# A hybrid transformer block on one core: the retention heads' gate columns and value columns change places in the program

## The chip, the cores and the metric

The kernel runs on one core of one Trainium2 chip. The metric is device time in microseconds (us) of one execution, given as the median of several runs. The engines are TensorE (PE, its weight loads shown as PEld), VectorE (DVE), ScalarE (ACT), GpSimd (POOL) and SyncE (SP). Each works through its own list of instructions in order, and semaphores make one wait for another; transfers are put in queues by SP and by ACT.

## The reference, cut to what matters

1024 latent tokens and 256 context tokens of width 1024 are normalised, modulated and projected by one matrix. Its columns go to two groups of heads:

```
p = h @ w_in                       # 1280 tokens x 4112 columns
qkv_a, z, ab, rq, rk, rv, rg = split(p)
# group A, gated delta rule: q, k, v after a 5-tap convolution and silu
q, k, v = silu(conv(qkv_a));  g = -exp(A) * softplus(a + dt);  beta = sigmoid(b)
o_gdn = rms_norm(delta(q,k,v,g) + delta_backward(...)) * silu(z)
# group B, retention: rotary on rq and rk, none on rv
o_ret = group_norm(ret(rq,rk,rv) + ret_backward(...)) * silu(rg)
x = x + g1 * (concat(o_gdn, o_ret)[latents] @ w_out)
x = x + g2 * swiglu(modulate(rms_norm(x)))
return rms_norm(x)
```

The columns rv (retention's values) are needed for all 1280 tokens, since the context's state starts the scan; the gates rg and z are needed for the latent tokens alone. Both have 512 columns, as have rk, rq and z. The 16 columns ab hold the decay and write strengths a and b of the delta rule and are needed for all tokens.

## The kernel before, in words

Each f32 operand is split into a high and a low part, and each product takes three matmuls. Tokens lie in 10 tiles of 128: tiles 0 and 1 are the context, tiles 2 to 9 the latents. A *token-major* product gives 128 tokens by 256 columns: `tm_half` (L367 to L373) issues 12 matmuls for half of the 1024 inputs, and a tile takes 24 in all. Ten groups of 256 columns are named by `GROUPS`, two to a name: groups 0 and 1 are rv, 2 and 3 rk, 4 and 5 rq, 6 and 7 rg, 8 and 9 z. Group 0 is 272 wide, because the 16 columns ab ride along; `tm_store` evacuates them to `xa` (L384), the rest to `res` (L402 or L532), and stores it in HBM. A *convolution block* (`conv_block`, L611 to L624) gives 128 columns by all tokens: 8 times 3 matmuls for each chunk of 256, 512 and 512 tokens, then two copies on ACT, shifted sums on DVE and a Silu on ACT.

The program's stages, with the microseconds of the profiled execution:

- 0 to 111, stage 1: the modulation's first rows, the norms (square root on ACT, L126), the transposes `xtr`, and groups 0 and 1 for all ten tiles, in the order of the tile groups 2-3, 4-5, 6-9, 0-1. Their evacuation is a plain copy. The PSUM banks for `tm` are three ("pa").
- 111 to 253: convolution blocks 4 to 7 (k) and 0 to 3 (q), with k's transposes `kt` for its norms. DVE runs `ada_rest` (sums `acc` over weights that SP loads, then a matmul `gr`, L504) and the softplus chain from `xa` to `g`; PE sums it up by `G` (L582) and transposes it by `GT` (L595). The result is needed for every chunk's decay.
- Groups 6 and 7 (rg, latents only, Silu on ACT) are written behind q. Their 384 matmuls lie in PE's list from 121 to 276.
- 277 to 377, preparation of the ten chunks: `pre(t)` loads k and q (`kc`, `qc`), multiplies them on PE (`kk` L705, `qt` L710, `kq` L715), loads the decay row `gw`, masks it on POOL, takes four exps on ACT (L726), and multiplies on DVE. `invert` runs 62 small steps on DVE for four chunks at once. Between these lie the convolution blocks 8 to 11 (v); each is followed by ten transposes `vT` (L856) of its result `y`, which ACT scales into `vt` (L859) and stores.
- 377 to 474: group 8 (z's first half) and the merges of the inverted blocks.
- After that the delta scan with groups 2 to 5 and 9 among it, the retention scan, the output projection and the feed-forward part, the last 750 us of it with PE busy nearly throughout.

The order of the instructions on each engine is not the order of the code. The code is written stage by stage, and a scheduler that works from estimated times moves the instructions of one stage between those of another wherever dependencies and buffers allow it; token-major groups fill PE's list in this way. Once compiled, each list is fixed.

Buffers matter too. Pool W holds the weights of the convolution blocks and of the late token-major groups (two buffers of each kind); pool W2, which is closed ahead of the preparation, holds those of group 1 and of rg.

Of the kernel before, what the change touches and what calls it, by code (L numbers as in the profile page):

```python
# [11 lines left out]
AF = mybir.ActivationFunctionType  # L12
# [13 lines left out]
H = 4  # L26
# [2 lines left out]
EPS = 1e-6  # L29
NEG = -200.0  # L30
FAR = -1e30
GROUPS = ["rv", "rk", "rq", "rg", "z"]


class Stop(Exception):
# [3 lines left out]
def build(nc, tc, ap, dbg=None, stop=None, marks=None):  # L39
    root = ExitStack()  # L40
    V, S, G, T, SY = nc.vector, nc.scalar, nc.gpsimd, nc.tensor, nc.sync

    def pool(name, bufs=1, side=None, space=None):
        kw = {}
        if side is not None:
            kw["side"] = side
        if space is not None:
            kw["space"] = space
        if space is not DRAM:
            kw["reuse_waits"] = "tile"  # L50
        es = ExitStack()
        p = es.enter_context(tc.tile_pool(name=name, bufs=bufs, **kw))
        root.push(es)
        p_close[id(p)] = es
        return p
# [3 lines left out]
    def close(p):  # L59
        p_close.pop(id(p)).close()  # L60
# [5 lines left out]
    def checkpoint(name):  # L66
        if dbg is not None:
            marks.append((name, int(nc.cur_bb.bb.instructions[-1].name.split("-")[-1])))
        if stop == name:
            raise Stop()  # L70
# [16 lines left out]
    def bank(tag, name):  # L87
        return PS["pool"].tile([P, 512], F32, tag=tag, name=name, bufs=PS["tags"][tag])

    def bank_a(name):  # L90
        return bank("pa", name)
# [99 lines left out]
    try:  # L191
# [20 lines left out]
        W = pool("w", bufs=2)  # L212
# [18 lines left out]
        WIDE = 272  # L231
        W2 = None
# [7 lines left out]
        def load_x(t):  # L240
            xts[t] = P0.tile([P, D], F32, tag="xt", name="xt", bufs=7)
            in_order(xts[t], ap["ctx"][t * P:(t + 1) * P, :] if t < 2 else ap["x"][(t - 2) * P:(t - 1) * P, :])
# [117 lines left out]
        def tm_weights(g, kh, pl, q=S):  # L360
            return weights(ap["wt"][g, :, 4 * kh:4 * kh + 4, :], [4, 256], V, pl, q, raws.get((g, kh)), g == 0)

        def tm_bank(g):
            return bank_a("tm")[:, 0:WIDE if g == 0 else 256]

        def tm_half(o, w, kh, t):

            tsl = slice(t * P, (t + 1) * P)
            whi, wlo = w
            for k in range(4 * kh, 4 * kh + 4):  # L370
                T.matmul(o, hhi[:, k, tsl], whi[:, k % 4, :], start=(k == 0), stop=False)  # L371
                T.matmul(o, hhi[:, k, tsl], wlo[:, k % 4, :], start=False, stop=False)  # L372
                T.matmul(o, hlo[:, k, tsl], whi[:, k % 4, :], start=False, stop=(k == KT - 1))  # L373
# [2 lines left out]
        zd = dr.tile([LT, P, 512], F32, tag="zd", name="zd")  # L376
        RD = {"rk": 0, "rq": 1, "rv": 2, "rg": 3}

        def tm_store(g, t, o, finish, store, pl):
            early = g < 2  # L380
            res = (W2 if early else R1).tile([P, 256], F32, tag="res", name="res", bufs=4 if early else 2)
            finish(t, o[:, 0:256], res)
            if g == 0:
                S.activation(xa[:, t, :], o[:, 256:WIDE], AF.Copy)  # L384
            nm, c0 = GROUPS[g // 2], (g % 2) * 256
            dst = zd[t - 2, :, c0:c0 + 256] if nm == "z" else rd[t, :, RD[nm], c0:c0 + 256]
            store.dma_start(dst, res)

        def token_major(g, tiles, finish, store, pl, q=S):

            w = [tm_weights(g, kh, pl, q) for kh in range(2)]

            for p in range(0, len(tiles), 2):
                pair = [(t, tm_bank(g)) for t in tiles[p:p + 2]]
                for kh in range(2):
                    for t, o in pair:
                        tm_half(o, w[kh], kh, t)
                for t, o in pair:
                    tm_store(g, t, o, finish, store, pl)

        def fin_copy(t, o, res):
            S.activation(res, o, AF.Copy)  # L402

        load_x(2)
        load_x(3)
# [18 lines left out]
        wr = {(0, 0): tm_weights(0, 0, W)}  # L424
# [22 lines left out]
        W2 = pool("w2", bufs=2)  # L447
        xa = W2.tile([P, TT, 16], F32, tag="xa", name="xa", bufs=1)
# [11 lines left out]
            hold = modulate(xnT[:, k, :], k, 0, slice(2 * P, 4 * P))  # L460
        normalize(1, hold)
        for gi, grp in enumerate(XGROUPS):
            for g in range(2):
                if gi == 0 and g == 1:
                    for kh in range(2):
                        wr[1, kh] = tm_weights(1, kh, W2)
                for t in grp:
                    if (g, t) in first:
                        o = first[g, t]
                    else:  # L470
                        o = tm_bank(g)
                        tm_half(o, wr[g, 0], 0, t)
                    tm_half(o, wr[g, 1], 1, t)
                    tm_store(g, t, o, fin_copy, S, W2)
                if g == 0 and gi + 1 < len(XGROUPS):
                    hold = modulated(gi + 1)
            if gi + 2 < len(XGROUPS):
                normalize(gi + 2, hold)
# [40 lines left out]
        def fin_rope(t, o, res):  # L519
# [7 lines left out]
                V.tensor_tensor(r4[:, :, a, :], o4[:, :, 1 - a, :], bc(sin, [P, 2, 64], 1), ALU.mult)  # L527
            for a, op in ((0, ALU.subtract), (1, ALU.add)):
                G.tensor_tensor(r4[:, :, a, :], ra[:, :, a, :], r4[:, :, a, :], op)

        def fin_gate(t, o, res):
            S.activation(res, o, AF.Silu)  # L532

        LAT, ALL = list(range(2, TT)), list(range(2, TT)) + [0, 1]
        for g in range(2):
# [66 lines left out]
        def conv_block(b, y, lat):  # L602

            whi, wlo = weights(ap["wg"][b], [KT, P], G if b % 2 else V, W, SY if b in (4, 5) else S)
            u = CV.tile([P, NTOK], F32, tag="u", name="u", bufs=2)
            for c0, n in (CHUNKS[1:] if lat else CHUNKS):
                ps = bank_c("b2")
                o = ps[:, :n]
                for k in range(KT):
                    hh, hl = hhi[:, k, c0:c0 + n], hlo[:, k, c0:c0 + n]  # L610
                    T.matmul(o, whi[:, k, :], hh, start=(k == 0), stop=False)  # L611
                    T.matmul(o, whi[:, k, :], hl, start=False, stop=False)  # L612
                    T.matmul(o, wlo[:, k, :], hh, start=False, stop=(k == KT - 1))  # L613
                S.activation(u[:, c0:c0 + n], o, AF.Copy)
                S.activation(y[:, c0:c0 + n], o, AF.Copy, scale=cw[:, b, 2:3])
            segs = [(NCTX, NLAT)] if lat else [(0, NCTX), (NCTX, NLAT)]
            for i, e in ((0, V), (1, V), (3, V), (4, V)):
                for s0, n in segs:
                    sh = i - 2
                    lo, hi = s0 + max(0, -sh), s0 + n - max(0, sh)  # L620
                    e.scalar_tensor_tensor(y[:, lo:hi], u[:, lo + sh:hi + sh], cw[:, b, i:i + 1], y[:, lo:hi],
                                           ALU.mult, ALU.add)
            a0 = NCTX if lat else 0
            S.activation(y[:, a0:], y[:, a0:], AF.Silu)  # L624

        def newy():
            return CV.tile([P, NTOK], F32, tag="y", name="y", bufs=3)
# [27 lines left out]
        for h in range(H):  # L655
            y = newy()
# [20 lines left out]
        for h in range(H):  # L677
            y = newy()
# [4 lines left out]
                        y[:, NCTX:].rearrange("p (t j) -> p t j", j=P))  # L683

        checkpoint("q")
        for g in (6, 7):
            token_major(g, LAT, fin_gate, S, W2, SY)
        checkpoint("rg")
        close(R2)
        close(W2)  # L690
        GU = pool("gu")
# [149 lines left out]
        def solve(b):  # L841
            for t in BATCH[b]:
                pre(t)
            checkpoint("pre%d" % b)
            invert(b)
            checkpoint("inv%d" % b)

        solve(0)
        solve(1)
        for h in range(H):  # L850
            y = newy()
            conv_block(8 + h, y, False)
            for t0, n in ((0, 2), (2, 4), (6, 4)):
                ps = bank_a("vT")
                for t in range(t0, t0 + n):
                    T.transpose(ps[:, (t - t0) * P:(t - t0 + 1) * P], y[:, t * P:(t + 1) * P], ident)  # L856
                vt = CV.tile([P, 4, P], F32, tag="vt", name="vt", bufs=2)
                for t in range(n):
                    S.activation(vt[:, t], ps[:, t * P:(t + 1) * P], AF.Copy, scale=sv3[:, t0 + t, h:h + 1])  # L859
                S.dma_start(vd[t0:t0 + n, :, h, :].rearrange("t p j -> p t j"), vt[:, :n])  # L860
        close(CV)
        checkpoint("v")
        RP = pool("rp", side="right")
# [12 lines left out]
        merge(2)  # L876


        for g in (8, 9):
            token_major(g, LAT, fin_gate, S, W)  # L880
        checkpoint("rgz")
        close(GM)
        close(G2)
# [374 lines left out]
        for i, l in enumerate(pairs):  # L1258
            y = nxt
# [194 lines left out]
        w = {}  # L1454
# [156 lines left out]
def prepare(inputs):  # L1611
# [13 lines left out]
    col = {"z": 1536, "rq": 2064, "rk": 2576, "rv": 3088, "rg": 3600}  # L1625
    wt = np.concatenate([w_in[:, col[n]:col[n] + 512] for n in GROUPS], 1)
    a["wt"] = f(wt.reshape(KT, P, 10, 256).transpose(2, 1, 0, 3))
# [27 lines left out]
```

## Time and profile before

| what | value |
|---|---|
| median of three runs | 1479.91 us (1479.66 to 1481.7) |
| the profiled execution | 1477.96 us |
| its span, first to last instruction | 1476.2 us |
| PE busy | 1397.2 us, 95% |
| DVE, ACT, POOL busy | 964.6, 614.0, 590.3 us |
| instructions | 24111, of them 8919 on PE |
| moved by DMA | 298.14 MB, 202 GB/s over the span |

The page gives busy times over the whole span and then the span in 40 slices, with a digit for each engine's tenths. The table of windows cuts it at given times. A row of the waits names the engine, what waits, `<-` what released it, and then the total, the count and the longest in us. In a timeline a row has its start, its length, the engine and the line of the program, then what is written `<-` what is read, and in square brackets the idle time ahead of it. "issue" is time in which the engine waited for nothing that the profile shows. Matmul records of f32 operands appear twice, since such a product takes two passes.

### The profile page before, as it was taken

The page shows a single profiled execution, that of the slowest core. Times are in us where ns is not written, and L with a number is a line of the kernel's source. Part 1 is how long each engine was busy: PE and PEld are TensorE (multiplying, and loading weights), DVE is VectorE, ACT ScalarE, POOL GpSimd, SP SyncE. Part 2 cuts the span into 40 slices and gives each one's busy share as a digit, 9 for nine tenths or more (in the row PEclk, how much of TensorE's full clock was granted, in tenths as well). Part 3 has the DMA queues.
Part 4 walks back from the last instruction along what each step waited for, and adds up shares of the span by engine and source line. Part 5 has one row for each costly group of instructions (what it writes and reads, how often), then busy time and mean ns, then how long its engine had stood idle before and what let it go on. Part 6 is the DMA issues. An engine that isn't in the chain of part 4 may idle for free.

```text
span 1476.2 us, 24111 instructions
## 1 busy us (share of the span) xinstructions
PE 1397.2 (95%) x8919; PEld 1199.2 (81%) x8919; DVE 964.6 (65%) x1856; ACT 614.0 (42%) x1326; POOL 590.3 (40%) x501
## 2 busy tenths in 40 slices
PE   7999999986789999899799899999999999999997
PEld 2898888975689999898688688877888888788885
DVE  6566789289792435689676877556555564657477
ACT  5643564587333111245443623233333332444445
POOL 0120010243202344234144688898555552335321
PEclk9999999998899999999899999999999999999999
DMA  9536686688888625996532265674222242776863
GB/s 337 197 105 205 189 249 200 219 264 277 282 216 277 238 76 178 416 341 209 184 125 104 97 238 210 242 264 162 105 97 105 107 151 79 260 260 194 288 216 114
DMA packets 170421, 298.14 MB, mean 202 GB/s; under 512 B 43496, under 2 KB 93880, under 8 KB 165952
## 3 DMA queue, kind: packets, MB, share of 16 engines
q1 hardware_dynamic: 118752, 253.17, 50.2%
q10 hardware_dynamic: 49072, 35.83, 7.8%
q0 software_dynamic: 2480, 7.60, 1.4%
q8 instruction: 70, 1.15, 0.3%
q14 instruction: 47, 0.39, 0.1%
HBM read 206.60 MB, written 89.96 MB: 201 GB/s over the span
## 4 chain that ended last, share of the span: by engine, by line
PE 55%; POOL 6%; DMA 5%; DVE 4%; issue 2%; ACT 2%; SPq 1%; ACTq 0%; POOLq 0%; DVEq 0%
PE ffn L1344 7%; PE ffn L1342 6%; PE ffn L1343 6%; PE fo L1470 4%; PE fo L1469 4%; PE fo L1468 4%; PE tm L371 3%; PE tm L373 3%; PE tm L372 3%; PE op L1203 2%; PE op L1201 2%; PE op L1202 2%; DMA wd<-tw 2%; POOL ws L1315 1%; DMA pk<-sd 1%
## 5 line engine op out<-in xcount | busy, mean ns | idle before, releaser
L371 PE MATMUL tm<-whi,hhi 128*128 128x256 f32 (+1 forms) x704 | 199.5, 287 | 7.7 <-ACT vt L859 3.4
L372 PE MATMUL tm<-wlo,hhi 128*128 128x256 f32 (+1 forms) x704 | 199.3, 285 | 2.4 <-issue 2.0
L373 PE MATMUL tm<-whi,hlo 128*128 128x256 f32 (+1 forms) x704 | 197.7, 285 | 0.0
L371 PEld LDWEIGHTS tm<-whi,hhi 128*128 128x128 f32 x704 | 132.8, 190 | 11.8 <-ACT vt L859 3.6
L1342 PE MATMUL ffn<-t,whi 128*128 128x512 f32 x352 | 136.9, 390 | 1.3 <-ACT whi L344 1.3
L1344 PE MATMUL ffn<-t,wlo 128*128 128x512 f32 x352 | 137.0, 390 | 1.0 <-DVE wlo L345 1.0
L1343 PE MATMUL ffn<-t,whi 128*128 128x512 f32 x352 | 137.0, 389 | 0.0
L372 PEld LDWEIGHTS tm<-wlo,hhi 128*128 128x128 f32 x704 | 133.7, 190 | 2.1 <-issue 0.9
L373 PEld LDWEIGHTS tm<-whi,hlo 128*128 128x128 f32 x704 | 132.8, 190 | 2.6 <-issue 1.8
L344 ACT ACTIVATE whi<-wraw 128x512 fp32r<-128x512 f32 (+2 forms) x98 | 75.1, 771 | 141.4 <-PE ffn L1343 80.5
L344 ACT ACTIVATE whi<-ws 128x512 fp32r<-128x512 f32 x88 | 55.6, 632 | 171.5 <-PE ffn L1343 123.4
L345 DVE TENSOR_TENSOR wlo<-ws,whi 128x512 fp32r<-128x512 f32 x88 | 93.9, 1068 | 47.0 <-ACT whi L344 46.8
L1469 PE MATMUL fo<-wlo,ahi 128*128 128x512 f32 x308 | 120.2, 390 | 2.1 <-DVE wlo L345 2.1
L1468 PE MATMUL fo<-whi,ahi 128*128 128x512 f32 x308 | 119.3, 390 | 0.7 <-ACT ahi L344 0.7
L1470 PE MATMUL fo<-whi,alo 128*128 128x512 f32 x308 | 119.0, 390 | 0.0
L345 DVE TENSOR_TENSOR wlo<-wraw,whi 128x512 fp32r<-128x512 f32 (+2 forms) x92 | 99.4, 1082 | 24.6 <-ACT whi L344 24.6
L1342 PE MATMUL ffn<-b,whi 128*128 128x512 f32 x264 | 103.8, 393 | 4.4 <-ACT whi L344 4.4
L1344 PE MATMUL ffn<-b,wlo 128*128 128x512 f32 x264 | 103.6, 393 | 0.8 <-DVE wlo L345 0.8
L1343 PE MATMUL ffn<-b,whi 128*128 128x512 f32 x264 | 103.4, 392 | 0.0
L612 PE MATMUL b<-hlo,whi 128*128 128x512 f32 (+1 forms) x256 | 94.4, 369 | 0.0
L613 PE MATMUL b<-hhi,wlo 128*128 128x512 f32 (+1 forms) x256 | 94.3, 368 | 0.0
L611 PE MATMUL b<-hhi,whi 128*128 128x512 f32 (+1 forms) x256 | 94.3, 368 | 0.0
(446 smaller groups left out, 3448.1 us busy)
## 6 DMA issues: line engine op xcount, KB each, us to landing
adaw<-ada SPq DMA_DIRECT2D x48, 512.0 KB, 4.4
pk<-sd SPq DMA_DIRECT2D x16, 1536.0 KB, 10.0
wraw<-wfi SPq DMA_DIRECT2D x44, 512.0 KB, 3.7
ar<-ad SPq DMA_DIRECT2D x33, 512.0 KB, 4.7
w<-wfo SPq DMA_DIRECT2D x22, 512.0 KB, 5.7
wd<-tw SPq DMA_DIRECT2D x11, 1024.0 KB, 4.8
ad<-act SPq DMA_DIRECT2D x20, 512.0 KB, 3.0
raw<-wd SPq DMA_DIRECT2D x20, 512.0 KB, 4.9
```

What stands on the lines that cost most here:

```text
L344: S.activation(hi, raw, AF.Copy)
L345: e.tensor_tensor(lo, raw, hi.bitcast(F32), ALU.subtract)
L371: T.matmul(o, hhi[:, k, tsl], whi[:, k % 4, :], start=(k == 0), stop=False)
L372: T.matmul(o, hhi[:, k, tsl], wlo[:, k % 4, :], start=False, stop=False)
L373: T.matmul(o, hlo[:, k, tsl], whi[:, k % 4, :], start=False, stop=(k == KT - 1))
L612: T.matmul(o, whi[:, k, :], hl, start=False, stop=False)
L1342: T.matmul(o, whi[:, k, :], xhi(xn, slice(0, 4), k), start=(first and k == 0), stop=False, **kw)
L1343: T.matmul(o, whi[:, k, :], xlo(xn, slice(0, 4), k), start=False, stop=False, **kw)
L1344: T.matmul(o, wlo[:, k, :], xhi(xn, slice(0, 4), k), start=False, stop=(k == 3), **kw)
L1468: T.matmul(po[g][i], ahi[:, ts], whi, start=(j == 0 and not kw), stop=False, **kw)
L1469: T.matmul(po[g][i], ahi[:, ts], wlo, start=False, stop=False, **kw)
L1470: T.matmul(po[g][i], alo[:, ts], whi, start=False, stop=(j == FH - 1), **kw)
```

## The change

Five things are done together. `GROUPS` now begins with rg and has rv in fourth place, so groups 0 and 1 are the gate, and 6 and 7 the values. Stage 1 computes groups 0 and 1 for the eight latent tiles alone and evacuates them with Silu (`fin_gate`); for the two context tiles it multiplies only the 16 columns ab, in 48 matmuls with 16 columns. The two groups behind q are gone. The value groups stand in the preparation, group 6 between `solve(0)` and `solve(1)` and group 7 behind convolution block 8, for all tiles, with weights in pool W. And the transposes of v are written one block later, the last ones behind group 8, which has moved ahead of the merges in the code.

```diff
-GROUPS = ["rv", "rk", "rq", "rg", "z"]
+GROUPS = ["rg", "rk", "rq", "rv", "z"]
...
-        def tm_half(o, w, kh, t):
+        def tm_half(o, w, kh, t, cols=slice(None)):
...
-            whi, wlo = w
+            whi, wlo = (x[:, :, cols] for x in w)
...
+        def gate_columns(t, o):
+            S.activation(xa[:, t, :], o, AF.Copy)
...
+        def fin_gate(t, o, res):
+            S.activation(res, o, AF.Silu)
...
         for gi, grp in enumerate(XGROUPS):
+            if grp[0] == 0:
+                for t in grp:
+                    o = bank_a("tm")[:, 0:16]
+                    for kh in range(2):
+                        tm_half(o, wr[0, kh], kh, t, slice(256, WIDE))
+                    gate_columns(t, o)
+                break
...
-                    tm_store(g, t, o, fin_copy, S, W2)
+                    tm_store(g, t, o, fin_gate, S, W2)
...
-        for g in (6, 7):
-            token_major(g, LAT, fin_gate, S, W2, SY)
-        checkpoint("rg")
...
-        solve(0)
-        solve(1)
-        for h in range(H):
-            y = newy()
-            conv_block(8 + h, y, False)
+        def vturn(h, y):
             for t0, n in ((0, 2), (2, 4), (6, 4)):
...
+        solve(0)
+        token_major(6, ALL, fin_copy, S, W, SY)
+        solve(1)
+        ys = []
+        for h in range(H):
+            ys.append(newy())
+            conv_block(8 + h, ys[h], False)
+            if h == 0:
+                token_major(7, ALL, fin_copy, S, W, SY)
+            else:
+                vturn(h - 1, ys[h - 1])
+        checkpoint("rv")
+        token_major(8, LAT, fin_gate, S, W)
+        vturn(H - 1, ys[H - 1])
...
-        for g in (8, 9):
-            token_major(g, LAT, fin_gate, S, W)
+        token_major(9, LAT, fin_gate, S, W)
```

What this does to the lists is seen at three places. First PE in the k stage, around the second `gr` and the sums `G` (names: `tm` a token-major product, `b_...` a convolution chunk). Before:

```order
L372 MATMUL tm<-wlo,hhi 128x256
L373 MATMUL tm<-whi,hlo 128x256
L371 MATMUL tm<-whi,hhi 128x256
L504 MATMUL gr<-acc,ones 1x512
L372 MATMUL tm<-wlo,hhi 128x256
L373 MATMUL tm<-whi,hlo 128x256
L371 MATMUL tm<-whi,hhi 128x256
L372 MATMUL tm<-wlo,hhi 128x256
L582 MATMUL G<-g,tri 128x40 x2
L583 MATMUL G<-g,ones 128x80
L373 MATMUL tm<-whi,hlo 128x256
```

The same place after the change:

```order
L621 MATMUL b_1330<-hhi,whi 128x512
L622 MATMUL b_1330<-hlo,whi 128x512
L623 MATMUL b_1330<-hhi,wlo 128x512
L517 MATMUL gr<-acc,ones 1x512
L592 MATMUL G<-g,tri 128x40 x2
L593 MATMUL G<-g,ones 128x80
L605 MATMUL GT<-ident,G 80x128
L621 MATMUL b_1357<-hhi,whi 128x512
L622 MATMUL b_1357<-hlo,whi 128x512
```

The gate products around `gr`, `G` and `GT` are gone from there; these stand directly behind one another, between two matmuls of convolution block 4's first wide chunk (`b_1330`) and its second (`b_1357`); another `gr` stands eleven matmuls earlier.

Second, PE at the end of the preparation. Before, the last chunk's products are followed by the last transposes of v and then by z's first half:

```order
L705 MATMUL kk<-kc 128x128 x4
L710 MATMUL qt<-ident,qc 128x128 x4
L715 MATMUL kq<-qc,kc 128x128 x4
L856 MATMUL vT<-ident,y 128x128 x10
L371 MATMUL tm<-whi,hhi 128x256
L372 MATMUL tm<-wlo,hhi 128x256
```

After:

```order
L371 MATMUL tm<-whi,hhi 128x256
L372 MATMUL tm<-wlo,hhi 128x256
L373 MATMUL tm<-whi,hlo 128x256
L859 MATMUL vT<-ident,y 128x128 x10
L371 MATMUL tm<-whi,hhi 128x256
L372 MATMUL tm<-wlo,hhi 128x256
```

The last transposes now stand behind the 192 matmuls of z's first half and ahead of 168 more token-major ones, which come before the first merge; the last chunk's products are further up.

Third, ACT in stage 1, around the square roots of the row norms (`rx2s`, `rx3s`). Before:

```order
L402 ACTIVATE res<-tm 128x256
L126 ACTIVATE rx2s<-ms,epsb 128x4
L387 DMA rd<-res 128x256 x3
L402 ACTIVATE res<-tm 128x256
L387 DMA rd<-res 128x256
L311 ACTIVATE hhi<-xtr,bmix,amix 128x512 x8
L325 ACTIVATE junk,ms<-xt 128x1024 x2
L126 ACTIVATE rx3s<-ms,epsb 128x2
L402 ACTIVATE res<-tm 128x256
```

After:

```order
L126 ACT_TABLE_LOAD
L126 ACTIVATE rx2s<-ms,epsb 128x4
L390 DMA rd<-res 128x256 x3
L408 ACT_TABLE_LOAD
L408 ACTIVATE res<-tm 128x256
L390 DMA rd<-res 128x256
L311 ACTIVATE hhi<-xtr,bmix,amix 128x512 x8
L325 ACTIVATE junk,ms<-xt 128x1024 x2
L126 ACT_TABLE_LOAD
L126 ACTIVATE rx3s<-ms,epsb 128x2
L408 ACT_TABLE_LOAD
L408 ACTIVATE res<-tm 128x256
```

Each square root has a table load ahead of it and one behind it, where the next evacuation is a Silu. On ACT as a whole there are 19 table loads after the change and 20 before. In the preparation, ACT's list has the 20 evacuations of value tiles between the exps of the chunks.

On PE, 195 matmuls of the value groups stand ahead of the first chunk's `kk`, where 384 of the gate groups stood; the other 285 stand among the chunks' products and the convolution blocks of v.

More of the change, by code (lines that the diff above doesn't have):

```diff
@@ L383, in tm_store @@
             if g == 0:
-                S.activation(xa[:, t, :], o[:, 256:WIDE], AF.Copy)
+                gate_columns(t, o[:, 256:WIDE])
             nm, c0 = GROUPS[g // 2], (g % 2) * 256
@@ L529, in fin_rope @@
                 G.tensor_tensor(r4[:, :, a, :], ra[:, :, a, :], r4[:, :, a, :], op)
-        def fin_gate(t, o, res):
-            S.activation(res, o, AF.Silu)
         LAT, ALL = list(range(2, TT)), list(range(2, TT)) + [0, 1]
```

## The prediction, made before the changed kernel was run

> **What bounds the kernel now.** I read the page's busy times and slices first, then a table of windows cut at the stage borders, then TensorE's waits in the windows where it idles, then timelines of single stretches.
>
> From the page:
>
> ```profile
> PE 1397.2 (95%) x8919; PEld 1199.2 (81%) x8919; DVE 964.6 (65%) x1856; ACT 614.0 (42%) x1326; POOL 590.3 (40%) x501
> ...
> PE   7999999986789999899799899999999999999997
> PEclk9999999998899999999899999999999999999999
> L371 PE MATMUL tm<-whi,hhi 128*128 128x256 f32 (+1 forms) x704 | 199.5, 287 | 7.7 <-ACT vt L859 3.4
> ```
>
> TensorE (PE) is busy 95% of the span, so time is lost or won almost only where it waits, or where its clock falls. One slice is 36.9 us; the digits fall in the ninth to eleventh, about 300 to 404 us, the clock digit with them. The stages the change touches, by windows (start and end; then busy us and instructions of each engine, clock, DMA share, GB/s):
>
> ```profile
> core 0: us, PE busy (x) PEld busy (x) DVE busy (x) ACT busy (x) POOL busy (x), PEclk, DMA share, GB/s
> 112.00:139.00 27.00, 27.00 (x192) 23.94 (x191) 20.30 (x46) 9.94 (x18) 0.00 (x0) 1.00 0.72 240
> 139.00:253.00 114.00, 114.00 (x606) 96.26 (x606) 92.81 (x159) 60.05 (x179) 9.58 (x4) 1.00 0.70 213
> 253.00:277.00 24.00, 24.00 (x196) 22.93 (x196) 6.90 (x12) 8.66 (x18) 1.76 (x3) 1.00 0.47 143
> 277.00:300.00 23.00, 23.00 (x144) 20.38 (x143) 13.35 (x16) 16.56 (x51) 9.61 (x13) 1.00 0.79 265
> 300.00:340.00 40.00, 34.63 (x210) 29.15 (x209) 33.52 (x53) 34.81 (x93) 17.20 (x15) 1.00 0.87 270
> 340.00:377.00 37.00, 21.01 (x114) 18.30 (x113) 34.70 (x49) 28.72 (x83) 15.19 (x12) 0.79 0.82 264
> 377.00:404.00 27.00, 23.62 (x194) 23.41 (x193) 20.19 (x54) 5.06 (x14) 4.67 (x4) 0.97 0.92 294
> 404.00:474.00 70.00, 62.22 (x1442) 58.56 (x1440) 44.18 (x114) 23.47 (x43) 6.83 (x13) 0.98 0.86 233
> ```
>
> From 112 to 300 PE is busy without a break (k and q convolutions, with the gate columns as filling). The chunk preparation (277 to 377) starves it: idle 5.37 in 300:340 and 15.99 in 340:377. In 377:404 it is idle 3.38, so 24.74 us over 300:404. The lower clock adds 21.01 × 0.21 + 23.62 × 0.03 = 5.1. The hole costs 29.8 us. The merges (404:474) lose 7.78 idle and 62.22 × 0.02 = 1.2, together 9.0. What PE waited for in 300:404 (total, times, longest):
>
> ```profile
> PE vT L856 <- ACT y L624: 9.6, 2, 9.3
> PE kk L705 <- issue: 8.4, 3, 6.7
> PE tm L371 <- ACT vt L859: 3.4, 1, 3.4
> PE qt L710 <- issue: 1.9, 1, 1.9
> ```
>
> **The change part by part.** The forecast is made against the profiled execution, 1477.96 us (span 1476.2, 1.76 around it). The median shown, 1479.91, is 1.95 above, and I add that at the end. A measurement of this kernel can tell about 0.2%, or 3 us, from no change.
>
> *PE's amount of work.* Before, the three token-major lines issue 704 each, 2112. After, stage 1 issues 384 gate matmuls and 48 narrow ones, the value columns 480, and the other columns 1248: again 2112 wide ones, with 48 narrow ones on top. The nearest price below is the merge stage's mean, 62.22 / 1442 = 0.043 us, mostly 32-wide work; above it a full matmul, 24.00 / 196 = 0.122. So 48 cost between 2.1 and 5.9; I take 3, since 16 columns stand nearer to the 32-wide row.
>
> *The hole filled.* Of the value columns, 195 matmuls stand ahead of the first chunk's product and 285 inside the preparation: 285 × 0.122 = 35 us of work that waits for nobody, against 29.8 of hole. The transposes one block later take away the 9.6 on y (ACT's Silu after the shifted sums), and the first half of z ahead of the last transposes takes away the 3.4 on vt. The kk and qt waits, 8.4 + 1.9 = 10.3, I leave standing: they are the chunk chain itself (load, POOL's mask, ACT's exp, DVE's product), which the filling does not shorten. It gives ACT 20 more evacuations, each behind its tile's last matmul with exps queued behind it. DVE, at 34.70 of 37 us, stays nearly full, and the four splits of the value weights are added to its queue. Bounds: 0, if the filling covers each wait, to 25, if it displaces the chain as much as it fills. The merges keep 7 of their 9.0: their own chain is untouched, and z's second half still stands there. For the clock and the joins I leave 3. Left over: 10.3 + 7 + 3, about 20 of the 38.8 (29.8 + 9.0).
>
> *ACT in stage 1.* Silu in place of Copy puts a table load beside each square root of the row norms. Rows of ACT's timeline, the two roots and the one load that stage 1 has before; then one PE wait of the first 112 us:
>
> ```profile
> 65.81 0.33 ACT L126 ACTIVATE rx2s<-ms,epsb 128x4 f32<-128x4 f32 x1
> 82.31 0.30 ACT L126 ACTIVATE rx3s<-ms,epsb 128x2 f32<-128x2 f32 x1
> ...
> 97.75 1.28 ACT L566 ACT_TABLE_LOAD   x1 [0.39 <-ACT res L402]
> 99.05 0.21 ACT L566 ACTIVATE nA<-alog 128x8 f32<-128x8 f32 x1
> ```
> ```profile
> PE tm L371 <- ACT xa L384: 1.9, 3, 1.3
> ```
>
> A load takes 1.28, up to 1.67 with the 0.39 ahead of it. One stands ahead of rx2 and delays the rows that the next transposes need. Two stand around rx3, ahead of an evacuation that PE's three banks wait for: PE already lost 1.9 to such evacuations, so there is no slack in the banks. The load behind rx2 meets ACT's own idle time and costs nothing. Three loads on the path make 3.8, with the 0.39 each 5.0, without any 0. I take 4. The Trainium skill, "ScalarE: Activation LUTs", section "What ACT_TABLE_LOAD costs", puts a switch at 1283 ns plus a drain of about 1380 ns, which speaks against a Silu among the roots; as an estimate by that page the three would cost 8.0 and the forecast would come out 4 later. The trace agrees on the 1.28 but shows 1.30 (99.05 − 97.75) from the load's start to the next activation and only 0.39 ahead of it.
>
> *The k stage loses its filling.* This is the term that I trust most. PE is in order. Rows of PE, then of DVE:
>
> ```profile
> 120.70 0.39 PE L613 MATMUL b<-hhi,wlo 128*128 128x512 f32 x1
> 127.25 1.02 PE L504 MATMUL gr<-acc,ones 128*1 128x512 f32 x2
> ```
> ```profile
> 124.85 0.75 DVE L499 SCALAR_TENSOR_TENSOR acc<-adaw,csl,acc 128x512 f32<-128x512 f32 x1
> ...
> 125.99 0.23 DVE L573 TENSOR_TENSOR g<-sps,nA 128x80 f32<-128x80 f32 x1
> ...
> 129.61 0.31 DVE L585 COPY G<-G 128x40 f32<-128x40 f32 x2 [0.23 <-PE G L583]
> ```
>
> Before, the convolution's first wide chunk ended at 120.70 + 0.23 = 120.93, and gate matmuls covered the time to gr at 127.25, whose operand was done at 124.85 + 0.75 = 125.60. After, gr stands two matmuls ahead of the chunk's end, with nothing between. PE is there earlier by the context tiles' 96 matmuls (11.7) and later by the narrow ones (3) and stage 1 (4): 120.93 − 0.46 − 11.7 + 3 + 4 = 115.8. DVE's chain hangs on its own DMAs and earlier rows and does not move up, so PE idles 125.6 − 115.8 = 9.8. Then G's transpose, now right behind G, waits for DVE's copies of G: 0.23 of waiting and 0.31 for them before, and with the row's sum that stands ahead of them on DVE I take 1. Around such an idle stretch the clock falls, as the preparation shows (start, length):
>
> ```profile
> 375.06 2.39 PE L856 MATMUL vT<-ident,y 128*128 128x128 f32 x10 [9.27 <-ACT y L624]
> 377.10 0.56 PE L371 MATMUL tm<-whi,hhi 128*128 128x256 f32 x1
> 377.46 0.41 PE L372 MATMUL tm<-wlo,hhi 128*128 128x256 f32 x1
> 377.67 0.41 PE L373 MATMUL tm<-whi,hlo 128*128 128x256 f32 x1
> ...
> 378.62 0.28 PE L372 MATMUL tm<-wlo,hhi 128*128 128x256 f32 x1
> 378.74 0.28 PE L373 MATMUL tm<-whi,hlo 128*128 128x256 f32 x1
> ```
>
> After 9.27 idle, work starts 0.21 apart instead of 0.12 until shortly ahead of 378.62: some 3.4 us from 375.06, nearly half of it lost, 2 with rounding. Between 139 and 253 the filling goes too (of one of the three lines):
>
> ```profile
> L371 PE MATMUL tm<-whi,hhi 128*128 128x256 f32 x23 | 6.5, 280 | 0.0
> ```
>
> With 23 + 21 + 21 = 65 such matmuls, 65 × 0.122 = 7.9 us of cover go from in front of the transposes kt and the later sums gr. DVE, which feeds both, is at 92.81 of 114 there. Between 0 and 7.9 I take 3.5. The k stage: 9.8 + 1 + 2 + 3.5 = 16.3; from 8, if DVE's chain comes up by half, to 21.
>
> *Queues.* The value weights' loads go to SP's and ACT's queues and share two buffers with the convolution's; a load that waits for a buffer holds the loads behind it. That lies in the 10.3 and its upper bound.
>
> *Sum.* Added or left: 3 + 4 + 16.3 + 20 = 43.3. Before: 38.8. Net +4.5, so 1482.4 profiled and, with 1.95, 1484 us.
>
> **The rivals.**
>
> *F, faster: the 35 us of filling cover the whole preparation.* Place: kk and qt of the last chunks. The chain starts earlier by the context tiles' 11.7 and by 189 fillings fewer ahead of it (384 against 195, 23.1), less the 23.3 of the three terms above: some 11 us, so it may be ahead of PE all through, the clock then stays at 1.00, and the 10.3 and 3 go, with 4 of the merges'. 1484 − 17 = 1467. It decides from the point where less than 13 of the 20 are left. For it: 35 exceeds 29.8. Against it: DVE's 34.70 of 37, and ACT in order.
>
> *N, stalls only move.* DVE's sums come up or the preparation leaves 15 rather than 20: 1479 to 1482, within 0.2%.
>
> *S, slower by 1%: the chain becomes the bound.* ACT waits for POOL already:
>
> ```profile
> L726 ACT ACTIVATE e<-e,nG 128x128 f32<-128x128 f32 x72 | 23.1, 392 | 11.8 <-POOL e L722 11.7
> ```
>
> If evacuations that stand behind a convolution's matmuls hold the exps of every chunk, the 10.3 become its upper bound, 25: 1499.
>
> *The change doesn't do what it says*: the order of PE shows the gate columns in stage 1 and the value columns beside kk, so this has no chance worth a number.
>
> **How the numbers follow.** The forecast's case (1483 to 1491) has 0.36, S 0.12, N 0.19, F 0.33. So slower by over 0.2%: 0.48; within: 0.19; faster: 0.33. Cases of both signs hold most of the chance: the forecast's own range is 1483 to 1491; the whole range, from just below F's 1467 to S's 1499, is 1466 to 1499. Beyond it lies F with the k stage's lower bound, or S with its upper one.
>
> **What would show each step.** Right, if in the new profile PE idles 8 to 12 us ahead of the second gr, the clock dips there, 300:404 holds no wait of vT for y, and waits of kk and qt come to about 10. Wrong, if the gr wait is under 4 (DVE's sums moved up), if kk and qt wait under 3 (F), or if waits of kk on ACT or POOL come to over 20 (S). Stage 1's term is wrong if PE's waits for res and xa stay at 1.9.

## The result: 1.1% slower, and the profile after

The changed kernel takes 1496.37 us in the median (1494.58 to 1499.83) against 1480.16 for the kernel before; the ratio is 1.0111, 95% interval 1.0090 to 1.0132. A second set of runs gave 1.0114 (1.0093 to 1.0136). The profiled execution is the longest of the first set, 1499.83 us, 21.9 above the profiled one of before; the medians differ by 16.2, so some 5.7 of these are scatter between executions. The ledger below is therefore one of places, and what an edit is worth is taken from the timed runs.

From the page of the changed kernel: engines, and PE's busy and clock digits in 40 slices.

```profile
PE 1413.7 (94%) x8967; PEld 1213.5 (81%) x8967; DVE 959.6 (64%) x1856; ACT 612.9 (41%) x1325; POOL 590.5 (39%) x501
...
PE   7897999988988999999799899999999999999997
...
PEclk9997999999999999999899999999999999999999
```

The hole of the ninth to eleventh slice has become shallower and longer, and there is a new dip in PE and its clock in the fourth, at about 112 to 150 us. The windows of the changed kernel, cut at the corresponding places (same columns as in the prediction):

```profile
60.00:107.20 47.20, 41.46 (x317) 39.42 (x316) 23.47 (x46) 29.94 (x57) 10.52 (x10) 0.96 0.21 68
107.20:114.00 6.80, 6.80 (x50) 6.80 (x49) 3.69 (x6) 2.53 (x4) 0.00 (x0) 0.76 0.59 176
114.00:140.10 26.10, 15.26 (x60) 10.39 (x60) 20.17 (x48) 4.40 (x11) 2.38 (x1) 0.70 0.54 175
140.10:267.50 127.40, 127.39 (x704) 108.76 (x705) 96.92 (x169) 62.83 (x183) 9.43 (x8) 0.98 0.72 213
267.50:401.50 134.00, 118.87 (x782) 107.89 (x780) 102.42 (x175) 83.36 (x237) 45.04 (x40) 0.96 0.75 232
401.50:428.60 27.10, 24.56 (x192) 24.36 (x193) 20.38 (x49) 8.15 (x18) 3.55 (x2) 0.94 0.90 262
428.60:452.00 23.40, 21.75 (x182) 21.08 (x180) 17.84 (x46) 6.31 (x18) 0.00 (x0) 1.00 0.87 250
452.00:520.00 68.00, 64.02 (x1449) 60.32 (x1450) 19.61 (x48) 18.82 (x33) 19.05 (x37) 0.95 0.67 201
```

The second row is the 48 narrow matmuls, the third the k stage up to the transpose of G, the fourth the rest of k and q, the fifth the preparation; then come z's first half, 168 more fillings and the merges. Counted as in the prediction (idle, plus busy time times the missing clock), the last four rows lose 15.1 + 4.8, 2.5 + 1.5, 1.7 and 4.0 + 3.2: 32.8 us, where the kernel before lost 38.8. So from the first kk to the last merge 6 less is lost. Ahead of it stand the narrow row with 6.8, 10.8 + 4.6 in the third and 2.5 in the fourth, where the kernel before lost nothing. With the 7.5 by which stage 1 ends later (next section) that makes 26.3 in all, and the first matmul `ffn` of the feed-forward part does start 25.9 later (868.0 against 842.1). At the last `ffn` it is 25.5 (1281.6 against 1256.1); behind it, in code that is the same, the profiled execution of before took 3.8 longer than this one.

What PE waited for in the changed kernel's preparation (267 to 402):

```profile
PE kk L712 <- ACT qt L719: 5.6, 2, 5.1
PE qt L717 <- issue: 3.7, 2, 2.7
PE vT L859 <- ACT y L634: 2.9, 1, 2.9
PE vT L859 <- ACT res L405: 1.2, 1, 1.2
PE kk L712 <- DMA kc<-sd: 0.7, 1, 0.7
PE tm L371 <- ACT vt L862: 0.5, 1, 0.5
```

The transposes' 9.6 have become 2.9 + 1.2, and kk and qt wait 10.0 in all, about as before, though 5.6 of it is now for a copy on ACT (`qt`). The value columns themselves (`tm`) wait hardly at all there. In the next stretch, 402 to 452, `tm` waits 3.0 for ACT's `res` and 1.3 for its `vt`.

### The profile page after: what moved, and what is told of

It is laid out like the page before. It is cut to its first block, busy times and chain, and to the rows that moved or that the text cites. A ratio compares the mean times of both kernels' runs of the same rounds, so it can differ in the third digit from the quotient of the medians.

```text
span 1497.9 us, 24228 instructions
## 1 busy us (share of the span) xinstructions
PE 1413.7 (94%) x8967; PEld 1213.5 (81%) x8967; DVE 959.6 (64%) x1856; ACT 612.9 (41%) x1325; POOL 590.5 (39%) x501
## 4 chain that ended last, share of the span: by engine, by line
PE 52%; POOL 7%; DMA 6%; DVE 4%; issue 4%; ACT 1%; SPq 0%; ACTq 0%; POOLq 0%; DVEq 0%
PE ffn L1361 6%; PE ffn L1359 6%; PE ffn L1360 6%; PE fo L1485 5%; PE fo L1487 5%; PE fo L1486 5%; PE tm L371 3%; PE tm L372 3%; PE tm L373 3%; DMA wd<-tw 2%; PE op L1218 2%; PE op L1220 2%; PE op L1219 2%; POOL ws L1332 2%; DMA sd<-vt 1%
## 5 line engine op out<-in xcount | busy, mean ns | idle before, releaser
L371 PE MATMUL tm<-whi,hhi 128*128 128x256 f32 (+2 forms) x720 | 206.2, 290 | 11.0 <-ACT xa L380 5.0
L372 PE MATMUL tm<-wlo,hhi 128*128 128x256 f32 (+2 forms) x720 | 206.4, 288 | 0.5 <-DVE wlo L345 0.5
L373 PE MATMUL tm<-whi,hlo 128*128 128x256 f32 (+2 forms) x720 | 204.1, 288 | 0.0
L371 PEld LDWEIGHTS tm<-whi,hhi 128*128 128x128 f32 x720 | 138.8, 194 | 13.7 <-ACT xa L380 5.7
L372 PEld LDWEIGHTS tm<-wlo,hhi 128*128 128x128 f32 x720 | 139.5, 194 | 2.6 <-issue 1.5
L373 PEld LDWEIGHTS tm<-whi,hlo 128*128 128x128 f32 x720 | 138.9, 194 | 0.6 <-DVE hlo L314 0.2
```

## Stage 1 and the k stage, row by row

ACT's timeline in stage 1 (start, length), the first square root in the kernel before, and then the changed kernel:

```profile
46.74 0.28 ACT L126 ACTIVATE rx1s<-ms,epsb 128x2 f32<-128x2 f32 x1
```
```profile
48.21 0.29 ACT L126 ACTIVATE rx1s<-ms,epsb 128x2 f32<-128x2 f32 x1
48.52 1.28 ACT L408 ACT_TABLE_LOAD   x1
...
68.21 1.28 ACT L126 ACT_TABLE_LOAD   x1
69.50 0.30 ACT L126 ACTIVATE rx2s<-ms,epsb 128x4 f32<-128x4 f32 x1
69.82 1.28 ACT L408 ACT_TABLE_LOAD   x1
...
85.96 1.28 ACT L126 ACT_TABLE_LOAD   x1
87.26 0.29 ACT L126 ACTIVATE rx3s<-ms,epsb 128x2 f32<-128x2 f32 x1
87.57 1.28 ACT L408 ACT_TABLE_LOAD   x1
```

Each load takes 1.28, and the next activation starts 1.29 or 1.30 behind the load's start (69.50 − 68.21, 87.26 − 85.96). The Trainium skill, "ScalarE: Activation LUTs", section "What ACT_TABLE_LOAD costs", gives the same 1283 ns and some 1380 ns of drain on top; no such second part shows in these rows. rx3s starts at 87.26 where it started at 82.31, 4.95 later, and the wide matmuls of the latent tiles end at 107.18 where they ended at 99.63, 7.55 later. Not all of this is the loads' doing: 1.47 (48.21 − 46.74) lies ahead of the first of them, and rx1s scatters as much between kernels whose stage 1 is the same (46.74 in the kernel before, 48.02 with the later transposes alone). So the switch to Silu makes 6.1. A part of it is PE's wait for evacuations into xa, 1.9 before:

```profile
PE tm L371 <- ACT xa L380: 5.0, 3, 2.7
```

PE's timeline in the narrow matmuls behind it:

```profile
107.32 0.26 PE L373 MATMUL tm<-whi,hlo 128*128 128x16 f32 x1
107.43 0.26 PE L371 MATMUL tm<-whi,hhi 128*128 128x16 f32 x1
...
111.06 0.36 PE L372 MATMUL tm<-wlo,hhi 128*128 128x16 f32 x1
111.27 0.36 PE L373 MATMUL tm<-whi,hlo 128*128 128x16 f32 x1
```

A matmul with 16 columns follows the last at 0.11 us, hardly faster than one with 256 (0.12); each has its own load of 128 by 128 weights. And after 3.7 us of them, with PE never idle, they follow at 0.21: the granted clock is 0.50 from 110.7 on, and stays there for the first 3.4 us of the convolution that follows. The Trainium skill, "TensorE: Matmul & The Clock Gate", section "LDWEIGHTS (loading the stationary operand)", says that a load takes its number of columns divided by 1.2 GHz; as an estimate by that, 128 columns take 107 ns. The 0.11 at the full clock agrees; the 0.21 at the halved one is twice that.

Then DVE's first sum, before and after, and the sum and the second gr that follow in the changed kernel:

```profile
99.37 0.48 DVE L497 TENSOR_SCALAR acc<-adaw,csl 128x512 f32<-128x512 f32 x1
```
```profile
106.92 0.48 DVE L510 TENSOR_SCALAR acc<-adaw,csl 128x512 f32<-128x512 f32 x1
...
132.38 1.54 DVE L512 SCALAR_TENSOR_TENSOR acc<-adaw,csl,acc 128x512 f32<-128x512 f32 x2 [1.18 <-DMA adaw<-ada]
```
```profile
134.07 1.86 PE L517 MATMUL gr<-acc,ones 128*1 128x512 f32 x2 [8.61 <-DVE acc L512]
```

The sums begin 7.55 later (106.92 against 99.37), because they stand behind stage 1's last rows on DVE, and end at 133.9, 8.3 later than the 125.6 of before. PE waits 8.61 for them all the same: both the one that waits and what it waits for have moved. PE comes to the second gr at 134.07 − 8.61 = 125.46. From 146 to 267.5 it is busy without a break at a clock of 1.00.

## The experiments

All times are set beside the kernel before on the same chip. Where matmuls are counted ahead of the chunks or among them, it is the token-major ones (`tm`) between the first convolution and the first kk, and between the first kk and the last.

**Copy in place of Silu in stage 1.** The gate is left without its Silu; PE's list stays the same.

```
-                    tm_store(g, t, o, fin_gate, S, W2)
+                    tm_store(g, t, o, fin_copy, S, W2)
```

> The changed kernel with a plain copy in place of Silu in stage 1, so that the gate is left without its Silu and no table load stands beside the square roots. Theory A (the loss starts in stage 1: the loads delay the row norms, DVE's sums start only when stage 1 is through, and PE waits bare for them): stage 1 ends 6 to 8 us earlier, the second gr comes earlier by as much, and the time falls from 1496 to 1488-1490. Theory B (the loss is in the preparation, where ACT's evacuations and the shared weight buffers hold the chunks): stage 1's gain is swallowed by the wait for the sums, 1494-1496. By the prediction's own term (4 us) it would be 1492.

Measured: 1489.6, ratio 1.0072 (1.0058 to 1.0086), 5.8 us less than the changed kernel by the ratios (2 to 9). In its profile the convolutions start at 105.45 instead of 114.05 (0.9 of that lies ahead of rx1), and PE's wait for the second gr is 10.0. So the loads delay stage 1, and most of the delay reaches the end; theory B, which had it swallowed, does not hold here.

**The same price in the kernel before.** Silu instead of the copy in stage 1, nothing else; the values then pass through a Silu that does not belong there.

```
-                    tm_store(g, t, o, fin_copy, S, W2)
+                    tm_store(g, t, o, fin_silu, S, W2)
```

> The kernel before with Silu in place of the copy in stage 1 and nothing else changed (its values rv are wrong by that Silu): the price of the table loads where the k stage has its filling. Theory A (the delay passes whole to the end, because PE is busy from stage 1 to the preparation): 5 to 7 more than before, 1485-1487. The prediction's term: 4 more, 1484. Rival (the preparation's stalls swallow it, since the chunk chain is late anyway): within 2 of before.

Measured: 1485.61, ratio 1.0045 (1.0031 to 1.0060), 6.7 us more. The convolutions start at 119.35 instead of 111.37; 1.9 of these 8.0 lie ahead of rx1, so the loads make 6.1. The preparation does not swallow the delay: it is paid in full.

**The sums moved behind q.**

```
-        for g in range(2):
-            ada_rest(2, g)
...
-            if h < 2:
-                ada_rest(5, h)
+            ada_rest(5 if h < 2 else 2, h % 2)
```

> The changed kernel with the sums of ada_rest for its first two halves moved from behind stage 1 to behind the convolution blocks of q. Theory A: PE no longer waits 8.6 us for the second gr, the clock does not fall for 17 us there, G waits a few us at most for the softplus chain; 10 us less, 1485-1488. Theory B: the wait was no loss, because the preparation is bound by the chunk chain, whose start depends on G; at most 3 less, 1493-1496.

Measured: 1492.07, ratio 1.0087 (1.0073 to 1.0102), 3.6 less than the changed kernel (0 to 7). Theory A's 10 were too many, though the 8.6 are gone: PE now waits 2.7 ahead of G in its place. Theory B's "at most 3" is not excluded either. The edit also changed the list: 312 value matmuls stand ahead of the chunks and 168 among them, where the changed kernel has 195 and 285. So the 3.6 are not the price of the wait alone. From the first kk to the last merge:

```profile
285.10:393.10 108.00, 94.54 (x639) 86.16 (x638) 70.53 (x117) 77.89 (x220) 38.72 (x35) 0.95 0.82 257
393.10:436.50 43.40, 38.26 (x312) 36.77 (x311) 35.97 (x92) 19.17 (x43) 7.99 (x6) 1.00 0.87 273
436.50:508.50 72.00, 64.83 (x1449) 61.00 (x1447) 36.49 (x92) 19.29 (x34) 16.08 (x31) 0.95 0.79 217
```

Idle and clock together lose 33.7 there, about as much as with 285 matmuls among the chunks (32.8).

**Both edits together.**

> The changed kernel with both edits of before: a plain copy in stage 1 (the gate is left without Silu) and the first sums of ada_rest behind q. Alone they took 6 and 4 us off. Theory A1 (two separate delays on PE's path): they add, 1485-1487. Theory A2 (the wait for gr is only what stage 1's delay did to DVE's sums): they overlap, 1489-1491.

Measured: 1485.24, ratio 1.0041 (1.0025 to 1.0056), 10.4 less than the changed kernel. The two gains add (A1); A2's 1489 to 1491 lie outside the interval. What is left of the loss is 6 us.

**The narrow matmuls, doubled and widened.** On top of both edits, once the 48 narrow ones issued twice, once with all 272 columns.

```
-                    for kh in range(2):
+                    for kh in (0, 1, 0, 1):
```
```
-                    o = bank_a("tm")[:, 0:16]
+                    o = bank_a("tm")[:, 0:WIDE]
...
-                        tm_half(o, wr[0, kh], kh, t, slice(256, WIDE))
-                    gate_columns(t, o)
+                        tm_half(o, wr[0, kh], kh, t)
+                    gate_columns(t, o[:, 256:WIDE])
```

> The kernel with both edits (copy in stage 1, sums behind q; 1485) and the 48 matmuls with 16 columns issued twice: the price of 48 more. By the prediction's price, 0.063 each, 3 more: 1488. By the changed kernel's trace (0.111 each as long as the clock is whole, 0.21 once it is halved), 5.4 to 10 more: 1491-1495.

> The kernel with both edits (1485) and the context tiles' 48 matmuls done with all 272 columns instead of 16 (the other 256 columns are thrown away): 17 times the columns. If the narrow ones are bound by their weights (theory E), it costs 48 x 0.015 = 0.7 more at full clock and gains what the clock lost to them: within 2 of 1485. By the prediction's price, 3 more: 1488.

Measured: doubled 1499.0, ratio 1.0136 (1.0118 to 1.0154), 14 more than both edits alone, above both forecasts; widened 1486.83, ratio 1.0060 (1.0044 to 1.0077), 2.8 more, which the intervals do not tell from none, nor from the 3 of the prediction's price. The windows over the stretch of these matmuls and, where there are 48, the start of the convolutions behind it. With 96 narrow ones:

```profile
100.02:105.10 5.08, 5.08 (x48) 5.08 (x46) 2.69 (x5) 0.38 (x1) 0.00 (x0) 0.99 0.64 181
105.10:115.86 10.76, 10.76 (x53) 10.76 (x52) 4.03 (x5) 1.24 (x2) 0.00 (x0) 0.50 0.36 124
```

With 48 narrow ones (both edits):

```profile
99.83:105.61 5.78, 5.78 (x50) 5.78 (x49) 3.05 (x5) 1.62 (x3) 0.00 (x0) 0.91 0.64 184
105.61:111.58 5.97, 5.97 (x27) 5.78 (x28) 5.97 (x10) 1.62 (x4) 2.41 (x1) 0.52 0.40 119
```

With 48 wide ones:

```profile
101.15:107.20 6.05, 6.05 (x50) 6.05 (x49) 2.70 (x5) 1.63 (x3) 0.00 (x0) 1.00 0.64 190
107.20:110.97 3.77, 3.58 (x28) 3.14 (x27) 3.77 (x5) 1.29 (x3) 2.36 (x1) 1.00 0.37 113
```

Ninety-six take 15.84 with 16 columns, 10.1 of the 14 that doubling costs; where the rest arises is not shown. Forty-eight take 5.78 with 16 columns and 6.05 with 272. The narrow ones pull the clock down to 0.50 in the midst of unbroken work, and the next convolution pays for it (0.52 over 5.97 us, against 1.00 over 3.77 for about as many matmuls). Leaving 256 columns out has saved no time that these runs can show on these two tiles.

**The later transposes alone, and the swap without them.** The first is the kernel before with the part of the diff from `vturn` on but without the value groups; the second is the changed kernel with this:

```
+            vturn(h, ys[h])
             if h == 0:
                 token_major(7, ALL, fin_copy, S, W, SY)
-            else:
-                vturn(h - 1, ys[h - 1])
...
-        token_major(8, LAT, fin_gate, S, W)
-        vturn(H - 1, ys[H - 1])
...
-        token_major(9, LAT, fin_gate, S, W)
+        for g in (8, 9):
+            token_major(g, LAT, fin_gate, S, W)
```

> The kernel before with one part of the change alone: the transposes of v one block later and the first half of z ahead of the last of them. Theory A: this part is the one that gains, by the two waits of the transposes for y and of tm for vt, 9.6 + 3.4: 1467-1472. Theory B: kk and qt wait in their place, the chunk chain sets the end of the preparation: 1477-1480.

> The changed kernel without the later transposes: the columns change places as they do, the transposes of v stand behind their own block and both halves of z behind the merges' code, as before. Theory A: the waits for y come back in part, 5 to 10 more, 1501-1506. Theory B: the value columns already cover those waits, within 3 of 1496.

Measured: the transposes alone 1476.67, ratio 0.9985 (0.9974 to 0.9996), 2.2 less, the only version that beats the kernel before, and only just; the swap alone 1512.68, ratio 1.0230 (1.0214 to 1.0246), 18 more than with the transposes. PE's longest waits with the transposes alone, and the wait of ACT behind the first of them:

```profile
PE tm L371 <- ACT res L532: 8.6, 4, 6.8
PE m L814 <- issue: 3.9, 1, 3.9
PE kk L705 <- issue: 3.5, 2, 1.9
PE vT L852 <- ACT y L624: 3.5, 1, 3.5
```
```profile
ACT res L532 <- DMA zd<-res: 26.1, 6, 13.9
```

and with the swap alone:

```profile
PE vT L859 <- ACT y L634: 14.9, 3, 11.7
PE kk L712 <- ACT qt L719: 8.5, 1, 8.5
```

In the kernel before, the later transposes bring the waits for y from 9.6 to 3.5, and others appear: the filling that is to cover them waits for its own evacuation (6.8 until 416.28), and that, at 415.85, has waited 13.9 for a buffer whose store had not landed. In the swap, the waits for y are 14.9, so there the later transposes are worth far more. Theory B was nearer for the first (1477 to 1480), theory A had the sign for the second, with 5 to 10 where 18 came.

**Only half of the gate columns in the preparation**, in the kernel before with the later transposes; stage 1 as it was.

```
-        for g in (6, 7):
-            token_major(g, LAT, fin_gate, S, W2, SY)
+        token_major(6, LAT, fin_gate, S, W2, SY)
...
         solve(0)
+        token_major(7, LAT, fin_gate, S, W, SY)
         solve(1)
```

> The kernel before with the later transposes and only the second half of the gate columns in the preparation, between the two solves; stage 1 and the first half stay as before, so PE keeps 192 fillings in the k stage and gets 192 in the preparation. Theory A (the loss of the change lies ahead of the chunks, the filling of the preparation is good): 8 to 12 less than with the later transposes alone, 1465-1469. Theory B (the chunk chain sets the length of the preparation, and filling only lengthens it): within 3 of 1477. Silu among the exps costs table loads on ACT: if they count, 1480 or more.

Measured: 1479.61, ratio 1.0009 (0.9992 to 1.0027): no gain over the kernel before, and none over the later transposes alone (0.9985), where theory A had 8 to 12. Ahead of the chunks PE loses nothing: it is busy without a break, at a clock of 1.00, from 111.8 to 264. But the list is not the one that the edit was to give. The token-major matmuls alone, ahead of the chunks and among them (busy time of PE, PEld, DVE, ACT, clock; the count of weight loads, PEld, is the exact one):

```profile
111.80:264.63 152.83, 41.92 (x331) 40.66 (x329) 0.00 (x0) 5.36 (x14) 1.00 0.68 208
264.63:368.20 103.57, 7.37 (x57) 6.66 (x55) 0.00 (x0) 1.15 (x4) 0.93 0.78 247
```

Of the 192 that were to go among the chunks, 55 stand there; the scheduler left the other 137 ahead of the first kk. So theory B's number is met and theory A's is not, but the run does not test the filling of the preparation. The third expectation, that table loads among the exps count, is not excluded: ACT has 24 loads here and 22 with the later transposes alone, 2 × 1.28 = 2.6 us.

**Less work on DVE in the preparation**, in the changed kernel and in the kernel before: three of the four shifted sums of v are left out.

```
-            for i, e in ((0, V), (1, V), (3, V), (4, V)):
+            for i, e in ((0, V), (1, V), (3, V), (4, V))[:1 if b >= 8 else 4]:
```

> The changed kernel with one of the four shifted sums of the v blocks 8 to 11 left out of four kept, that is, only the first is done (v is wrong by the other three); some 18 us of DVE's work go from the preparation, PE's list stays the same. Theory C (DVE, in order, paces the chunks: banks and buffers come free only when it is through, so the filling moves PE's waits instead of covering them): the loss between the first kk and the last merge falls from 36-39 us to about 20, time 1478-1484. Rival D (the chain of load, mask and exps on POOL, ACT and DMA paces it): within 4 of 1496.

> The kernel before with the same three sums of v left out. Theory C: DVE paces its preparation too, 10 to 16 less than 1480, 1464-1470. Rival D: within 4 of 1480.

Measured: 1502.9, ratio 1.0173 (1.0148 to 1.0199), and 1487.34, ratio 1.0062 (1.0046 to 1.0077): both some 9 us *slower*, with DVE 19 to 20 us less busy. Theory C's times are not met. The lists did not stay the same as I had expected: the scheduler packs PE's list anew, from 306 us on in the changed kernel and from 260 in the kernel before, so the runs do not test DVE's work alone. In the changed kernel without the three sums, the preparation and the stretch to the first merge:

```profile
267.30:393.80 126.50, 117.79 (x780) 107.00 (x779) 90.26 (x174) 84.93 (x236) 41.90 (x40) 0.97 0.81 246
393.80:456.10 62.30, 49.47 (x373) 48.45 (x371) 29.57 (x71) 15.00 (x39) 3.55 (x2) 0.89 0.82 231
```

and what PE waited for most there, with ACT's wait behind it:

```profile
PE tm L371 <- ACT vt L862: 12.8, 4, 5.3
```
```profile
ACT vt L862 <- DMA sd<-vt: 15.7, 2, 9.1
```

The preparation is shorter by 7.5 (126.50 against 134.00), so DVE's work may well count there; the stretch behind it loses all of that and more (62.30 against 50.50), at waits for stores of vt. The two profiled executions take the same in all (1499.54 and 1499.83), so they do not show where the 9 us of the timed runs lie. What the profiles do show is that the stall moves with each edit: to ACT's y, to its res or to its vt, the last two behind a store that holds one of two buffers.

## Why the prediction came out as it did

Slower was forecast, with a chance of 0.48 against 0.33 for faster, and slower it is. The time lay in the whole range (1466 to 1499), but beyond the forecast's own case (1483 to 1491): of the loss, 4 us were forecast and 16 measured. What reached up to 1496 in the range was rival S, whose mechanism did not occur, so that the range held the time is luck. Step by step:

- **The hole filled** is the term of the sum that was mis-sized most: 20 of 38.8 were to be left over, 32.8 are. Its first part held in size: kk and qt wait 10.0, against 10.3 forecast, and the merges lose 7.2, against 7. "For the clock and the joins I leave 3" failed: in place of 3 there are 15.6, made of vT's 2.9 + 1.2, z's and the next fillings' 5.7, 4.8 of clock, and small stalls. So 35 us of work that waits for nobody did not fill a hole of 30, and with 168 matmuls among the chunks instead of 285 about as much was lost (33.7). Why is shown in part only. PE takes its list in order, and each filling has a fixed place in it; I take it that those which stand ahead of or behind a wait cannot cover it. Between the chunks the fillings wait only 0.5 themselves, behind them 4.3 for evacuations, and in other lists 8.6 and 12.8. No run has the filling without the rest of the change.
- **The amount of PE's work**: the price per narrow matmul was 0.063 and is 0.11, then 0.21: 6.9 us in place of 3, and half of the next 3.4 us on top, since the clock stays down: 1.7 more. I took the row that was nearest in columns (32 wide) where the nearest in weights (128 by 128) was wanted. Doubling them costs 14 in the timed runs, so the 3 were too little by far.
- **ACT in stage 1**: 4 forecast, 6.1 in the profile without the scatter ahead of the first load, 5.8 and 6.7 in the two timed edits. The three loads on the path are there with 1.28 each; the one behind rx1 was left out of the count, and the clock fell at the wait of 2.67 behind rx3 (272 columns follow at 0.23 instead of 0.12 from 90.24 to 93.62). The reason was right, the size too small; PE's wait for xa rose from 1.9 to 5.0, as the term's own sign asked.
- **The k stage** was forecast at 16.3; the windows show 10.8 + 4.6 + 2.5 = 17.9, of which 1.7 belong to the narrow matmuls' clock: 16.2. That the two agree is luck. The wait (9.8 forecast, 8.61 measured) has the size but not the reason: "DVE's chain ... does not move up" was true, and it moved back by 8.3, because it starts behind stage 1. I had let stage 1's delay shorten this wait; it did not. PE came to gr at 125.46 instead of 115.8, 9.7 later: 3.5 by stage 1, 3.9 and 1.7 by the narrow matmuls and the clock behind them, and 0.5 because gr stands behind the chunk's last matmul and not two ahead of it. The two errors cancel. The 3.5 for the lost cover between 139 and 253 are 0: all of the fourth row's 2.5 is the clock up to 146. In their place, G's copy took 0.7 of the 1 forecast, a wait for a convolution's evacuation on ACT 1.6, and the clock 5.4 where 2 were forecast. And only some 3.6 came back when the sums were moved, so a part of the wait would have been lost elsewhere.
- **Rivals**: F needed less than 13 us left over, far from 32.8. N's 1479 to 1482 is excluded by the interval. S has the nearest time, 1499, but not its mechanism: kk and qt wait no longer than before.
- **Signs**: the wait for gr, the clock's dip there and the 10 us of kk and qt came as named; that no vT waits for y between the chunks did not: 2.9 are left.

What stays open: what in the end sets the length of the preparation and of the fillings behind it. The three lists that are counted here all lose more than 30 there (38.8, 32.8, 33.7); whether more buffers for the evacuations, so that a store holds nobody, would free it was not tried. Why both kernels are slower with less DVE work is open too: their lists changed with it. Of the 6 us that are left with both edits, no run takes the narrow matmuls and the hole apart.

## What to carry to other kernels

Work that is to fill an idle engine can bring waits of its own: ask whether what it needs (banks, evacuations, stores) is free there as well, and read in the list where the scheduler has really put it. Taking it from a place where it covered a wait can uncover that wait. When a chain moves later at its start, a wait for it does not shrink because the waiting engine is late too: follow both ends. Price a small matmul with fresh weights by its weights, not by its columns. And look where a profile's delay begins: what lies ahead of the first changed instruction is not the change's doing.

## What the runs showed of the hardware that was not expected

A matmul with 16 columns and fresh 128 by 128 weights takes 0.11 us, one with 256 takes 0.12, and 48 with 272 columns took 6.05 us against 5.78 with 16. In the profiles here, a stream of the narrow ones lowers the granted clock to 0.50 within 3 to 5 us while PE is never idle (3.7 in the changed kernel, 5.0 in the doubled stream), and 96 of them took 15.84 us; with 272 columns it stays at 1.00.
